# One transformer layer on one core: the normalised rows of the mixing step in one tile per token half, and the operands of the branch products in those same places

## The chip, the cores and the metric

The kernel runs on one core of a Trainium2 chip. What counts is the device time of one execution in microseconds (us), and the time of the kernel before is the median of three runs. In the profile PE is TensorE (PEld its weight loads), DVE is VectorE, ACT is ScalarE, and SP is the queue that issues all DMAs here.

## The reference, cut to what matters

One layer with 1024 tokens and a width of 1024, in float32:

```
h  = x + 1/2 * SwiGLU_1(RMSNorm(x))
u  = RMSNorm(h)
[fox q,k,v,f | dsa q,k,v | indexer q,k,w | mem q | gates] = u @ W_in
o_A = forgetting attention (8 heads of 64)      # "fox", branch n = 0
o_B = top-k sparse attention (8 heads of 64)    # "sparse", branch n = 1
o_C = attention to 256 memory tokens (4 heads of 128)   # "mem", branch n = 2
h  = h + W_out( sum_n sigmoid(u W_g_n) * (o_n W_br_n) )
y  = h + 1/2 * SwiGLU_2(RMSNorm(h))
```

The part in question is the third line from the end: the gates (24 column blocks of `u @ W_g`), and the three branch products, in which each o_n has 512 rows and 1024 tokens.

## The kernel before

Each matrix product is made of three: operands are split into a high and a low part in fp32r (`split`, line 230: a copy on ACT writes the high part, a subtraction on DVE the low part), and `mm3` (line 317) adds high x high, high x low and low x high. A weight block comes by `weights` (line 250): a DMA of 512 KB into a staging slot `wS`, of which there are two during the attention and four once `open_more` has opened a second pool, then ACT's cast to `wH` and DVE's subtraction to `wL`. A slot comes free when that subtraction has read it.

The normalised rows u lie turned (features on partitions) in two tiles `uh` and `ul`, each 128 x 8 x 1024, together 64 KB of each partition, in the pool `u`. `norm_rows` (line 301) writes them, `Block.step` (line 336) and the gates read them.

The order of the work is set in the program by `_Flow.run`, which steps generators ("chains") one at a time by an estimated clock, and after that the framework's scheduler places the instructions of each engine. While the attention heads run, at most two at a time, a *filler* chain gives PE work between their steps: first the gates (`Gates.work`, 24 blocks in groups of two, for each group both blocks over the first 512 tokens, then both over the last 512, two steps for each block and half, 96 steps in all), then `fill` (line 1674). When the last gate is done, `fill` releases the pools of the selection, of the gates and of u, opens a pool `o` in their room, and loads the operands of branch 2 with `o_loaded` (line 1332): for k = 0 to 3 the reciprocal sums of the softmax by DMA into `oR`, the unnormalised o by DMA into `wS`, DVE's product of the two, and the split into high and low tiles of the pool `o`. Then `branch` (line 1293) runs the 16 products of branch 2 (tiles `br` in PSUM, four rows of the contraction with three products each, 12 matmuls), each weighted by its gate (`bg`, loaded from `g_s`) on DVE and stored to `mg_s`. Branch 0 follows in the same way once all fox heads are done, and adds what `mg_s` holds (`bm`). Branch 1 needs the last sparse head, so it runs after all heads, in `last_branch` (line 1741), with tiles of a pool `merge`, and writes its sums as split operands (`u2h`, `u2l`) of the product with W_out (`tm`).

How far the filler may run ahead of the heads is set by `pace`:

```
    left = 2 * 24 * 2 - gates_f.n + 40
    def pace():
        return fill_c.n <= min(left * (sum(c.n for c in heads) / total) + PACE, left - RESERVE)
```

with PACE 4 and RESERVE 6. The 40 are the steps of `fill` after the gates: four loads, 16 products, four loads, 16 products. The last six steps are so kept for the time when all heads are done.

Of the kernel before, what the change touches and what calls it, by code (L numbers as in the profile page):

```python
# [19 lines left out]
P = 128  # L20
# [135 lines left out]
def trunk_layer_kernel(  # L156
# [144 lines left out]
    def norm_rows(tp, row, gain, uh, ul, t, free=None, sq=None, **junk):  # L301
# [3 lines left out]
        for c in range(2):  # L305
            pt = free("nT") if free else bank("nT")
            for k in range(4):
                T.transpose(pt[:, k * P:(k + 1) * P], sq[:, (4 * c + k) * P:(4 * c + k + 1) * P], ident)
            keep = fl.t
            hs = uh[:, 4 * c:4 * c + 4, t * P:(t + 1) * P]  # L310
            ls = ul[:, 4 * c:4 * c + 4, t * P:(t + 1) * P]
            split(hs, ls, pt.rearrange("p (k t) -> p k t", k=4))
            if c == 0:
                fl.t = keep
# [7 lines left out]
    class Block:  # L322
# [13 lines left out]
        def step(self, uh, ul, t, consume, after=None):  # L336
# [7 lines left out]
            for k in range(NK):  # L344
                wh, wl = self.ws[k // kper]
                wh, wl = wh[:, k % kper], wl[:, k % kper]
                a, b = [x[:, k, t * P:(t + 1) * P] if not isinstance(x, list) else
                        x[t // 4][:, k, t % 4 * P:(t % 4 + 1) * P] for x in (uh, ul)]
# [12 lines left out]
    def block_chains(blocks, uh, ul, nt, deps=None, after=None):  # L361
        cs = []
        for i, (b, consume) in enumerate(blocks):
            nxt = blocks[i + 1][0] if i + 1 < len(blocks) else after
            order = getattr(consume, "order", range(getattr(consume, "first", 0), nt))
            for t in order:
                cs.append(chain(b.step(uh, ul, t, consume, nxt if t == order[-1] else None),
# [647 lines left out]
    class Gates:  # L1015


        def __init__(self, uh, ul):
            self.u, self.got, self.tp = (uh, ul), {}, None
# [6 lines left out]
        def work(self):  # L1026
            uh, ul = self.u
            self.fetch(0)
            self.fetch(1)
            for d0 in range(0, 24, 2):  # L1030
                for c, d in ((0, d0), (0, d0 + 1), (1, d0), (1, d0 + 1)):
# [5 lines left out]
                    for k in range(NK):  # L1037
                        if k == NK // 2:
                            yield
                        mm3(pt, [(wh[:, k], uh[:, k, sl]), (wh[:, k], ul[:, k, sl]), (wl[:, k], uh[:, k, sl])],  # L1040
                            k == 0, k == NK - 1)
# [251 lines left out]
    def branch(tp, n, os_, first, dst):  # L1293
# [6 lines left out]
        fetch(0)  # L1300
        fetch(1)
        for dp in range(4):
            fetch(dp + 2)
            wh, wl = got.pop(dp)
            for c in range(2):
                for d in (2 * dp, 2 * dp + 1):
# [18 lines left out]
                    else:  # L1325
                        hv, lv = dst[0][c][:, d], dst[1][c][:, d]
# [5 lines left out]
    def o_loaded(op, n, k):  # L1332
# [5 lines left out]
        return weights(o_s[n, k], [P, S], op, "o", 8, f)  # L1338
# [92 lines left out]
    def to_mix(t, free=None):  # L1431
# [3 lines left out]
        return norm_rows(m["np"], ff.h[t], m["gain"], m["uh"], m["ul"], t, free, stage)  # L1435


    def beside(i, y):
        m = mixing
        if i == 5:  # L1440
            m["up"] = pool("u", side="right")
            m["uh"], m["ul"] = [m["up"].tile([P, NK, S], F32R, name=n) for n in ("uh", "ul")]
# [13 lines left out]
        if i == 9:  # L1456
# [3 lines left out]
            m["gates"] = Gates(m["uh"], m["ul"])  # L1460
# [7 lines left out]
    up, uh, ul = mixing["up"], mixing["uh"], mixing["ul"]  # L1468
# [7 lines left out]
    nch = block_chains([(nb, narrow)], uh, ul, NT, [[]] * 4 + [[c] for c in norms])  # L1476
# [178 lines left out]
    chains = block_chains(blocks, uh, ul, NT)  # L1655
# [10 lines left out]
    right = {"up": up}  # L1666
# [7 lines left out]
    def fill():  # L1674
        yield from gates_f.gen
        finish(sel_c)
        sel.release()
        sgp.release()
        up.release()
        op = right["op"] = pool("o", side="right")  # L1680
        os_ = []
        for k in range(4):
            os_.append(o_loaded(op, 2, k))
            yield fl.clk["PE"] + 2.0
        yield from branch(op, 2, os_, True, None)
        os_ = []
        for k in range(4):
            while not foxes[2 * k + 1].done:
                yield fl.clk["PE"] + 1.0
            os_.append(o_loaded(op, 0, k))  # L1690
            yield fl.clk["PE"] + 2.0
        for t in branch(op, 0, os_, False, None):
            if len(b_os) < 4 and sparses[2 * len(b_os) + 1].done:
                b_os.append(o_loaded(op, 1, len(b_os)))
# [41 lines left out]
    up = pool("u2")  # L1736
    uh, ul = zip(*[[up.tile([P, NK, 512], F32R, name=f"u2{w}{c}") for w in "hl"] for c in range(2)])
    uh, ul = list(uh), list(ul)
    tp = pool("merge")

    def last_branch():
        while len(b_os) < 4:
            b_os.append(o_loaded(op, 1, len(b_os)))
# [7 lines left out]
    tp.release()  # L1751
    op.release()
    repartition(8)
# [41 lines left out]
    fl.run(block_chains(blocks, uh, ul, NT, after=Next()), width=4)  # L1795
    up.release()
# [49 lines left out]
```

## Time and profile before

| | |
|---|---|
| median of 3 runs | 2520.55 us (2514.85 to 2521.84) |
| the profiled execution, its own time | 2521.56 us |
| its span, first to last instruction | 2519.5 us |
| PE busy | 2419.0 us (96% of the span) |
| DVE busy | 1619.4 us (64%) |
| ACT busy | 1149.5 us (46%) |
| mean granted TensorE clock | 0.983 |

A row of the timeline gives the start, the length, the engine, the operation with what it writes and reads, and, in brackets, for how long the engine was idle before it and which event ended that. A row of stretches gives the busy time of each engine within a stretch of the span, and the granted TensorE clock there, where 1.00 is 2.4 GHz and 0.50 is 1.2 GHz. The heads and the gates take the span from about 1170 to 1707 us, the last branch lies between 1722 and 1766 us, and the product with W_out follows it.

### The profile page before, as it was taken

To read this page: it belongs to the slowest core of one execution; us is meant where nothing else is said; L and a number is where in the kernel's file an instruction comes from. 1 tells how busy PE (TensorE), PEld (TensorE's weight loads), DVE (VectorE), ACT (ScalarE), POOL (GpSimd) and SP (SyncE) were. 2 spreads that over 40 slices of the span, in tenths; PEclk is the share of its full clock that TensorE was granted. 3 is DMA by queue.
4 is the path that set the end of the run, shared out by engine and by line. 5 is a ranking of instruction groups with operands and counts; after the bars stand their busy time and mean duration, and the time that the engine had idled before them with its cause. 6 is when DMAs were issued, how large, how long until landed. Compare 5 with 4: busy or idle time off the path is not lost.

```text
span 2519.5 us, 31509 instructions
## 1 busy us (share of the span) xinstructions
PE 2419.0 (96%) x11532; PEld 1998.8 (79%) x11532; DVE 1619.4 (64%) x3162; ACT 1149.5 (46%) x1918; POOL 2.2 (0%) x40
## 2 busy tenths in 40 slices
PE   6999999999999999989999997999999999999998
PEld 5888888888788777777787886888777888888887
DVE  7665555488776788675565456787368555554885
ACT  6433333333443476768854554543144333333332
POOL 0000000000000000000000000000000000000000
PEclk9999999999999999999999998999999999999999
DMA  4323222484345434444554525757413222225743
GB/s 135 122 96 117 93 91 76 159 309 141 131 137 161 153 106 137 137 155 148 149 158 131 142 89 168 236 186 249 160 67 92 84 92 76 84 86 191 266 150 130
DMA packets 300922, 352.15 MB, mean 140 GB/s; under 512 B 19896, under 2 KB 202840, under 8 KB 300768
## 3 DMA queue, kind: packets, MB, share of 16 engines
q1 hardware_dynamic: 300768, 350.15, 43.5%
q8 instruction: 90, 1.47, 0.2%
q14 instruction: 64, 0.52, 0.1%
HBM read 255.51 MB, written 93.54 MB: 139 GB/s over the span
## 4 chain that ended last, share of the span: by engine, by line
PE 74%; DVE 11%; ACT 6%; DMA 6%; issue 3%; SPq 0%; ACTq 0%; DVEq 0%
PE gx L51 18%; PE gy L51 14%; PE tm L51 8%; PE dx L51 7%; PE gate L51 7%; PE dy L51 7%; PE br L51 3%; PE po L51 3%; ACT junk L51 2%; PE sp L51 2%; DVE wL L51 2%; PE pT L51 2%; DMA wS<-in_ffn_w_down 1%; PE nar L51 1%; PE kv L51 1%
## 5 line engine op out<-in xcount | busy, mean ns | idle before, releaser
L51 ACT CAST wH<-wS 128x1024 fp32r<-128x1024 f32 (+1 forms) x230 | 217.0, 949 | 300.3 <-PE gy L51 76.4
L51 DVE TENSOR_TENSOR wL<-wS,wH 128x1024 fp32r<-128x1024 f32 (+1 forms) x230 | 250.6, 1095 | 108.7 <-ACT wH L51 105.2
L51 PE MATMUL gx<-th,wH 128*128 128x512 f32 x704 | 222.7, 398 | 10.3 <-ACT wH L51 6.2
L51 PE MATMUL gy<-th,wH 128*128 128x512 f32 x704 | 221.1, 395 | 5.3 <-DVE th L51 3.5
L51 PE MATMUL gx<-raw,wH 128*128 128x512 f32 x704 | 217.0, 389 | 0.6 <-DVE gu L51 0.6
L51 ACT ACTIVATE junk<-wk,sn 128x384 bf16<-128x384 f32 (+5 forms) x186 | 164.3, 883 | 67.2 <-DVE sn L51 58.3
L51 PEld LDWEIGHTS gx<-th,wH 128*128 128x128 f32 x704 | 134.7, 192 | 40.5 <-ACT wH L51 7.4
L51 DVE TENSOR_TENSOR pl<-pT,ph 128x512 fp32r<-128x512 f32 (+1 forms) x176 | 109.8, 638 | 86.8 <-ACT ph L51 85.3
L51 ACT CAST wH<-S 128x1024 fp32r<-128x1024 f32 x88 | 92.2, 1052 | 158.5 <-PE gy L51 150.5
L51 PEld LDWEIGHTS gy<-th,wH 128*128 128x128 f32 x704 | 133.7, 191 | 34.8 <-DVE th L51 4.4
L51 PE MATMUL gate<-uh,wH 128*128 128x512 f32 x384 | 156.6, 408 | 0.0
L51 DVE TENSOR_TENSOR gu<-gu,gy 128x512 f32<-128x512 f32 x88 | 60.3, 686 | 148.1 <-PE gy L51 105.2
L51 DVE TENSOR_TENSOR wL<-S,wH 128x1024 fp32r<-128x1024 f32 x88 | 107.4, 1223 | 73.9 <-ACT wH L51 73.9
L51 PEld LDWEIGHTS gx<-raw,wH 128*128 128x128 f32 x704 | 132.0, 188 | 28.6 <-DVE gu L51 1.1
L51 PE MATMUL gate<-ul,wH 128*128 128x512 f32 x384 | 153.1, 399 | 0.0
L51 PE MATMUL gate<-uh,wL 128*128 128x512 f32 x384 | 152.3, 397 | 0.0
L51 PE MATMUL tm<-wH,uh 128*128 128x512 f32 x368 | 148.5, 405 | 3.3 <-ACT wH L51 3.3
L51 PE MATMUL tm<-wL,uh 128*128 128x512 f32 x368 | 146.1, 397 | 1.0 <-DVE wL L51 0.5
L51 PE MATMUL tm<-wH,ul 128*128 128x512 f32 x368 | 145.7, 396 | 0.0
L51 PE MATMUL dx<-wH 128*128 128x512 f32 x352 | 138.1, 392 | 2.7 <-DVE rows L51 2.6
L51 PE MATMUL gx<-th,wL 128*128 128x512 f32 x352 | 138.9, 395 | 0.6 <-DVE wL L51 0.5
L51 PE MATMUL gy<-th,wL 128*128 128x512 f32 x352 | 138.7, 394 | 0.0
(282 smaller groups left out, 5528.3 us busy)
## 6 DMA issues: line engine op xcount, KB each, us to landing
wS<-in_ffn_w_down SPq DMA_DIRECT2D x70, 512.0 KB
wS<-in_w_in SPq DMA_DIRECT2D x48, 512.0 KB
wS<-in_ffn_w_gate SPq DMA_DIRECT2D x46, 512.0 KB
wS<-in_ffn_w_up SPq DMA_DIRECT2D x44, 512.0 KB
hid_s<-gu SPq DMA_DIRECT2D x44, 512.0 KB
a<-hid_s SPq DMA_DIRECT2D x30, 512.0 KB
g_s<-sg SPq DMA_DIRECT2D x48, 256.0 KB
bg<-g_s SPq DMA_DIRECT2D x48, 256.0 KB
```

The source lines that it names most:

```text
L51: return fn(*a, **k)
```

## The change

- u lies in two tiles, `u0` for tokens 0 to 511 and `u1` for tokens 512 to 1023, each with both parts (128 x 2 x 8 x 512). A class `Rows` hands out the pieces that readers and writers took before.
- `Rows.again(c)` takes the place of half c a second time, as a tile 128 x 4 x 2 x 1024 for the four high and four low operands of a branch.
- `fill` counts the steps of the gates. After step 92 (the last two blocks over tokens 0 to 511 are done, and four steps over `u1` are left) it finishes the selection, releases its pool, opens the pool `o` and takes the place of `u0`. From there on each of the last four gate steps is followed by one `o_loaded` of branch 2, and the last of these by the first weight block of the branch. Branch 0's operands go to the place of `u1`, branch 1's to that of `u0` again. The loads of branch 2 are no steps of their own any more, and `pace` is as before.
- `branch` yields between its first and second weight block.
- The last branch uses the pool `o` for `bg` and `bm` instead of a pool `merge`; its result goes to a `Rows` pair, and the pools `o`, `sgp` and `u` are released after it.

```diff
+    class Rows:
+        def __init__(self, rp):
+            self.rp = rp
+            self.t = [rp.tile([P, 2, NK, 512], F32R, tag=f"u{c}", name=f"u{c}", bufs=1) for c in range(2)]
...
+        def again(self, c):
+            t = self.rp.tile([P, 4, 2, S], F32R, tag=f"u{c}", name="o", bufs=1)
+            return iter([(t[:, k, 0], t[:, k, 1]) for k in range(4)])
...
         fetch(0)
+        yield
         fetch(1)
...
-    def o_loaded(op, n, k):
+    def o_loaded(op, n, k, place):
+        keep = fl.t, fl.last
         f = op.tile([P, S], F32, tag="oR", name="oR", bufs=2)
...
-        return weights(o_s[n, k], [P, S], op, "o", 8, f)
+        hi, lo = next(place)
+        v = slot([P, S], F32, "wS")
+        load(v, o_s[n, k])
+        V.tensor_mul(v, v, f)
+        split(hi, lo, v)
+        fl.t, fl.last = keep
+        return hi, lo
...
     def fill():
-        yield from gates_f.gen
-        finish(sel_c)
-        sel.release()
-        sgp.release()
-        up.release()
-        op = right["op"] = pool("o", side="right")
-        os_ = []
-        for k in range(4):
-            os_.append(o_loaded(op, 2, k))
-            yield fl.clk["PE"] + 2.0
-        yield from branch(op, 2, os_, True, None)
+        n, os_ = gates_f.n, []
+        for t in gates_f.gen:
+            n += 1
+            if n == 2 * 24 * 2 - 4:
+                finish(sel_c)
+                sel.release()
+                op = right["op"] = pool("o", side="right")
+                first, places = branch(op, 2, os_, True, None), u.again(0)
+            if n >= 2 * 24 * 2 - 4 and len(os_) < 4:
+                os_.append(o_loaded(op, 2, len(os_), places))
+                if len(os_) == 4:
+                    next(first)
+            yield t
+        yield from first
...
-        yield from branch(tp, 1, b_os, False, (uh, ul))
+        yield from branch(op, 1, b_os, False, u2)
...
-    tp.release()
     op.release()
+    sgp.release()
+    up.release()
```

The instructions of each engine are the same in number and kind; their order is the same up to the last gates, and differs from there to the product with W_out.

The first place is DVE's order where the operands of branch 2 are made. Here `wS<-wS,oR` is the product with the reciprocal sums, `pl` the low part of a head's probabilities, `wL` the low part of a weight block or operand, `o` the operand's low part in its new place, `bg<-bg,br` the first use of a branch product. Before, from the last `pl` ahead of the first branch product:

```order
L51 TENSOR_TENSOR pl<-pT,ph 128x512
L51 RECIPROCAL sums<-sums 128x8
L51 TENSOR_TENSOR wS<-wS,oR 128x1024 x2
L51 TENSOR_TENSOR wL<-wS,wH 128x1024 x4
L51 SCALAR_TENSOR_TENSOR bg<-bg,br 128x512
L51 TENSOR_TENSOR wL<-wS,wH 128x1024
L51 SCALAR_TENSOR_TENSOR bg<-bg,br 128x512 x2
```

Changed, from the first operand on (the first two products with the sums lie 17 and 7 `pl` ahead of it):

```order
L51 TENSOR_TENSOR o<-wS,o 128x1024
L51 TENSOR_TENSOR pl<-pT,ph 128x512
L51 TENSOR_TENSOR pl<-pT,ph 128x384
L51 TENSOR_TENSOR o<-wS,o 128x1024
L51 TENSOR_TENSOR wS<-wS,oR 128x1024 x2
L51 TENSOR_TENSOR o<-wS,o 128x1024
L51 TENSOR_TENSOR pl<-pT,ph 128x384
L51 TENSOR_TENSOR pl<-pT,ph 128x512
L51 TENSOR_TENSOR o<-wS,o 128x1024
L51 TENSOR_TENSOR os<-po,lo 64x512
L51 TENSOR_TENSOR pl<-pT,ph 128x512
L51 TENSOR_TENSOR wL<-wS,wH 128x1024
```

The same operations stood together between the last gate and the first branch product; now they stand between the heads' own operations while the last four gate steps run on PE.

The second place is PE's order where the heads end. `po` are the last products of the last head, `rT` its sums, `br` a branch product. Before:

```order
L51 MATMUL rT<-ident,sums 8x128
L51 MATMUL br<-wH 128x512
L51 MATMUL br<-wL,wH 128x512
L51 MATMUL po<-pl,vs 128x256 x2
L51 MATMUL po<-ph,vs 128x256
L51 MATMUL po<-ph,vs 128x128
L51 MATMUL po<-pl,vs 128x256
L51 MATMUL po<-pl,vs 128x128
L51 MATMUL br<-wH,wL 128x512
```

Changed:

```order
L51 MATMUL rT<-ident,sums 8x128
L51 MATMUL br<-o,wH 128x512
L51 MATMUL po<-pl,vs 128x256 x2
L51 MATMUL po<-ph,vs 128x256
L51 MATMUL po<-ph,vs 128x128
L51 MATMUL po<-pl,vs 128x256
L51 MATMUL po<-pl,vs 128x128
L51 MATMUL br<-o,wH 128x512
```

From `rT` to the first `tm` there were 252 `br` matmuls, which is 21 tiles of 12; now there are 216, which is 18. Sixteen of them are branch 1, so five tiles of branch 0 were left behind the heads, and now two are.

The third place is SP's order at the same point, where the last operand of branch 1 (`wS<-o_s`) and the weights of branch 1 (`wS<-in_w_branch`) are loaded. Before:

```order
L176 DMA o_s<-os 64x512
L173 DMA oR<-r_s 64x1024
L176 DMA mg_s<-bg 128x512
L173 DMA wS<-o_s 128x1024
L173 DMA bm<-mg_s 128x512
L176 DMA mg_s<-bg 128x512
L173 DMA bg<-g_s 128x512
L173 DMA bm<-mg_s 128x512
L173 DMA wS<-in_w_branch 128x4x256
```

Changed:

```order
L176 DMA o_s<-os 64x512
L173 DMA oR<-r_s 64x1024
L173 DMA wS<-o_s 128x1024
L176 DMA mg_s<-bg 128x512
L173 DMA wS<-in_w_branch 128x4x256
L176 DMA mg_s<-bg 128x512
L173 DMA wS<-in_w_branch 128x4x256 x2
```

The first weight block stands behind one store of a branch product instead of two, and three blocks stand before any further `bg`.

## Rows read from the trace of the kernel before

**Rows 1.** Stretches from the last gates to the first branch products: the stretch and its length, busy time (and instructions) of PE, PEld, DVE, ACT and POOL, then the granted clock, the share of the DMA engines and GB/s.

```profile
1500.00:1525.00 25.00, 25.00 (x153) 21.84 (x152) 9.24 (x23) 10.64 (x25) 0.00 (x0) 1.00 0.14 48
1525.00:1545.00 20.00, 13.59 (x84) 11.41 (x82) 17.58 (x45) 13.37 (x28) 0.00 (x0) 0.92 0.53 151
1545.00:1557.00 12.00, 1.36 (x3) 1.00 (x4) 5.67 (x7) 4.18 (x7) 0.00 (x0) 0.50 0.81 262
1557.00:1600.00 43.00, 41.63 (x212) 34.74 (x211) 27.61 (x41) 15.56 (x23) 0.00 (x0) 0.94 0.78 242
```

**Rows 2.** PE's timeline: the end of the 92nd gate step, the end of the last gate, the three waits behind it, and the first head operation after the first 36 branch matmuls.

```profile
1507.91 0.39 PE L51 MATMUL gate<-uh,wL 128*128 128x512 f32 x1
...
1529.90 0.39 PE L51 MATMUL gate<-uh,wL 128*128 128x512 f32 x1
...
1541.59 0.63 PE L51 MATMUL po<-ph,vs 128*128 128x256 f32 x2 [3.53 <-ACT ph L51]
1545.24 0.79 PE L51 MATMUL po<-pl,vs 128*128 128x256 f32 x2 [3.03 <-DVE pl L51]
1556.43 0.79 PE L51 MATMUL br<-wH 128*128 128x512 f32 x1 [10.40 <-ACT wH L51]
...
1567.70 0.60 PE L51 MATMUL pT<-ident,ns 128*128 128x128 f32 x4
```

**Rows 3.** SP's queue in the same stretch: start, time to issue, what is loaded.

```profile
1531.82 0.92 SPq L173 DMA_DIRECT2D oR<-r_s  x2
...
1541.58 1.46 SPq L173 DMA_DIRECT2D wS<-o_s  x2
...
1551.58 1.59 SPq L173 DMA_DIRECT2D wS<-in_w_branch  x2
```

**Rows 4.** DVE's and, last, ACT's timeline in the same stretch.

```profile
1537.47 2.34 DVE L51 TENSOR_TENSOR wS<-wS,oR 128x1024 f32<-128x1024 f32 x2
1540.34 2.34 DVE L51 TENSOR_TENSOR wL<-wS,wH 128x1024 fp32r<-128x1024 f32 x2
...
1547.87 2.55 DVE L51 TENSOR_TENSOR wS<-wS,oR 128x1024 f32<-128x1024 f32 x2 [2.57 <-DMA wS<-o_s]
...
1555.34 1.04 ACT L51 CAST wH<-wS 128x1024 fp32r<-128x1024 f32 x1 [3.84 <-DMA wS<-in_w_branch]
```

**Rows 5.** Pieces of the chain of waits, start and length, that give the time of PE's work in steps: a gate step, transposes, products with the values, scores.

```profile
1508.30 0.44 PE pT L51 x4
1508.74 0.48 PE po L51 x4
...
1518.69 1.27 PE sp L51 x8
...
1521.28 2.76 PE gate L51 x12
```

**Rows 6.** ACT's timeline at the 92nd gate step: the gate's tanh.

```profile
1508.34 0.60 ACT L51 ACTIVATE sg<-gate 128x512 f32<-128x512 f32 x1 [2.64 <-PE gate L51]
```

**Rows 7.** PE's timeline where the heads end: the last product of the last head, and the first matmul of branch 1.

```profile
1708.02 0.39 PE L51 MATMUL po<-pl,vs 128*128 128x256 f32 x2
...
1722.60 0.50 PE L51 MATMUL br<-wH 128*128 128x512 f32 x1 [0.96 <-ACT wH L51]
```

**Rows 8.** SP's queue behind it: the last head's output stored and loaded again, and the first weights of branch 1.

```profile
1709.78 0.45 SPq L176 DMA_DIRECT2D o_s<-os  x1
...
1712.76 0.65 SPq L173 DMA_DIRECT2D wS<-o_s  x1
...
1716.28 0.46 SPq L173 DMA_DIRECT2D wS<-in_w_branch  x1
```

**Rows 9.** DVE's timeline there: the product with the sums, and the first use of a product of branch 1.

```profile
1717.30 1.23 DVE L51 TENSOR_TENSOR wS<-wS,oR 128x1024 f32<-128x1024 f32 x1 [0.38 <-DMA wS<-o_s]
...
1730.33 0.68 DVE L51 SCALAR_TENSOR_TENSOR bg<-bg,br 128x512 f32<-128x512 f32 x1
```

**Rows 10.** ACT's timeline there: the high part of the last operand, and of the first weight block.

```profile
1718.56 1.05 ACT L51 CAST wH<-wS 128x1024 fp32r<-128x1024 f32 x1 [9.53 <-DVE wS L51]
1721.50 1.04 ACT L51 CAST wH<-wS 128x1024 fp32r<-128x1024 f32 x1 [1.88 <-DMA wS<-in_w_branch]
```

**Rows 11.** PE's timeline at the end of branch 1: its last matmul, the two waits in the product with W_out, and the first matmul that takes 0.39 us again.

```profile
1766.06 0.39 PE L51 MATMUL br<-wH,wL 128*128 128x512 f32 x1
...
1773.21 0.49 PE L51 MATMUL tm<-wH,u2h 128*128 128x512 f32 x1 [2.68 <-ACT wH L51]
1774.73 0.80 PE L51 MATMUL tm<-wL,u2h 128*128 128x512 f32 x1 [1.03 <-DVE wL L51]
...
1780.82 0.39 PE L51 MATMUL tm<-wH,u2h 128*128 128x512 f32 x1
```

**Rows 12.** DVE's timeline at the same place: the last product of branch 1, and behind it the low part of W_out's fourth block.

```profile
1772.87 0.68 DVE L51 SCALAR_TENSOR_TENSOR bg<-bg,br 128x512 f32<-128x512 f32 x1
1773.46 1.22 DVE L51 TENSOR_TENSOR wL<-wS,wH 128x1024 fp32r<-128x1024 f32 x1
```

**Rows 13.** Stretches with the granted clock (columns as in the first group): two around the clock's return after the wait at the gates, and the one at and after the wait at W_out.

```profile
1560.00:1562.00 2.00, 2.00 (x6) 1.61 (x5) 1.16 (x1) 0.00 (x0) 0.00 (x0) 0.50 0.39 121
1562.00:1564.00 2.00, 2.00 (x9) 1.60 (x9) 1.41 (x2) 1.05 (x1) 0.00 (x0) 0.93 0.87 248
...
1774.00:1780.00 6.00, 5.26 (x12) 4.18 (x13) 1.97 (x3) 0.63 (x1) 0.00 (x0) 0.50 0.65 222
```

More of the change, by code (lines that the diff above doesn't have):

```diff
@@ L334, in fetch, with step @@
                     self.ready[j] = fl.arrival()
-        def step(self, uh, ul, t, consume, after=None):
+        def step(self, u, t, consume, after=None):
             self.fetch()
@@ L359, in col_srcs, with block_chains @@
         ]
-    def block_chains(blocks, uh, ul, nt, deps=None, after=None):
+    def block_chains(blocks, u, nt, deps=None, after=None):
         cs = []
@@ L366, in block_chains @@
             for t in order:
-                cs.append(chain(b.step(uh, ul, t, consume, nxt if t == order[-1] else None),
+                cs.append(chain(b.step(u, t, consume, nxt if t == order[-1] else None),
                                 deps[t] if deps and i == 0 else getattr(consume, "deps", ())))
@@ L1441, in beside @@
             m["up"] = pool("u", side="right")
-            m["uh"], m["ul"] = [m["up"].tile([P, NK, S], F32R, name=n) for n in ("uh", "ul")]
+            m["u"] = Rows(m["up"])
             m["np"] = pool("norm2")
@@ L1665, in trunk_layer_kernel @@
     masks = []
-    right = {"up": up}
+    right = {}
     def finish(c):
@@ L1689, in fill @@
                 yield fl.clk["PE"] + 1.0
-            os_.append(o_loaded(op, 0, k))
+            os_.append(o_loaded(op, 0, k, places))
             yield fl.clk["PE"] + 2.0
+        right["places"] = u.again(0)
         for t in branch(op, 0, os_, False, None):
             if len(b_os) < 4 and sparses[2 * len(b_os) + 1].done:
-                b_os.append(o_loaded(op, 1, len(b_os)))
+                b_os.append(o_loaded(op, 1, len(b_os), right["places"]))
             yield t
@@ L1735, in trunk_layer_kernel @@
     wx = more["pool"]
[L1736 to L1739, printed above, removed]
+    up2 = pool("u2")
+    u2 = Rows(up2)
     def last_branch():
         while len(b_os) < 4:
-            b_os.append(o_loaded(op, 1, len(b_os)))
+            b_os.append(o_loaded(op, 1, len(b_os), right["places"]))
         yield fl.clk["PE"] + 8.0
         yield lambda: fill_c.done
-        yield from branch(tp, 1, b_os, False, (uh, ul))
+        yield from branch(op, 1, b_os, False, u2)
     fl.run([chain(last_branch())], filler=fill_c)
@@ L1794, in trunk_layer_kernel @@
     blocks = [(Block(None, col_srcs(w_out, i * 512, 512), 512, 4), f) for i, f in enumerate((residual, normed_rows))]
-    fl.run(block_chains(blocks, uh, ul, NT, after=Next()), width=4)
-    up.release()
+    fl.run(block_chains(blocks, u2, NT, after=Next()), width=4)
+    up2.release()
     combos.open_high()
```

35 lines of the change are left out of this document (18 added, 17 removed).

## The prediction

> **What bounds the kernel now.** I read the stretches first. PE is busy 25.00 of 25 us while the last gates run, then only 13.59 of 20 and 1.36 of 12, and then nearly full again [rows 1]. So the place to look at is the 32 us between the last gates and the first branch products. PE's timeline shows three waits there, 3.53, 3.03 and 10.40 us long, 16.96 us together [rows 2]. The reader is to see what each waits for: a high part from ACT, a low part from DVE, and then the first weights of branch 2.
>
> SP's and DVE's timelines show why. The last gate ends at 1530.1 [rows 2], and only then may the pool of the operands open: the sums are issued at 1531.82 [rows 3], DVE's products with them run from 1537.47, 5.65 us later, and their casts and subtractions follow. Only the subtractions free the two staging slots, so the next two operands are issued at 1541.58 [rows 3] and multiplied from 1547.87, 6.29 us later [rows 4], and the weights, again in the same slots, come at 1551.58 and are cast at 1555.34, 3.76 us later [rows 3, 4]. That is three loads, one behind the other, 26 us from the last gate to the first branch matmul at 1556.43. The heads cover about 9 us of it. They can't cover more: PE takes its instructions in order, and DVE's low parts for the heads stand between the operands' products.
>
> The waits cost the clock as well. In 1545 to 1557 the granted clock is 0.50, the level of 1.2 GHz, and it is back only after 1562 [rows 1, 13]. The 36 branch matmuls from 1556.43 take until 1567.70 [rows 2], 11.3 us, where 12 take 2.76 us at the full clock [rows 5] and 36 would take 8.3. So another 3.0 us go there. The loss at the gates is 16.96 + 3.0 = **20.0 us**.
>
> The second place is the end of the heads. The last head's last product ends at 1708.4. Its output goes out to DRAM (issued 1709.78), comes back (issued 1712.76), is multiplied at 1717.30 and cast at 1718.56. The first weights of branch 1 are issued at 1716.28 and cast at 1721.50 [rows 7 to 10]. All that takes 14 us, and five tiles of branch 0, 5 x 2.76 = 13.8 us less the two matmuls already done, lie under it, so that PE waits 0.96 us alone [rows 7].
>
> The third place is the product with W_out: branch 1 ends at 1766.3, PE does 18 matmuls, then waits 2.68 and 1.03 us [rows 11], and runs at clock 0.50 until 1780.8 [rows 11, 13]. Fourteen matmuls in 6.1 us instead of 3.2 are 2.9 us. That loss is 3.71 + 2.9 = 6.6 us. It comes from DVE, which first uses a product of branch 1 at 1730.33 [rows 9], 7.7 us after PE began it, where a tile takes 2.76. DVE is thus 5 us late, and ends its last one at 1773.5 [rows 12], with the low part of W_out's fourth block behind it in order.
>
> **The change, part by part.** *u in two tiles.* The same instructions on the same sizes, in the same order up to the last gates. I cost it at nothing. It needs no cover.
>
> *The operands of branch 2 from gate step 92 on.* The sums and the first two operands are loaded well before, as the order of DVE shows. What remains starts when `u0` is dead, at 1508.1 [rows 2]. Then follow the step's tanh on ACT (0.60) [rows 6], the cast (1.05) [rows 10] and the subtraction (1.17, half of 2.34) [rows 4], which frees a slot at 1511.0. The third operand's load takes between 4.54 us (1712.76 to 1717.30) [rows 8, 9] and 6.29 us. The DMA engines are at a share of 0.14 there [rows 1], against 0.53 to 0.81 where the 6.29 was seen, so I take the lower: 1515.5. The fourth comes one subtraction later, 1516.7; product 1517.9; subtraction of the third 1519.0; weights 3.76 us later, 1522.8; cast 1523.9; low part 1525.1. With 6.29 for each of these loads it is 1529.4.
>
> PE's cover: between step 92 and the first branch matmul the new order has four gate steps, 25 transposes, 28 products with values and 8 scores: 4 x 2.76 + 25 x 0.11 + 28 x 0.12 + 8 x 0.16 = 18.4 us [rows 5], so it gets there at 1526.5. That is 1.4 us behind the low part, or 2.9 us ahead of it at the other end. DVE's products now stand between the heads' low parts, but each of these is used a gate step later, 2.76 us, about what one late load costs. I put **1.5 us** of new waits here, half of the worse end. Removed: 20.0. Balance 18.5.
>
> *The four steps fewer.* `pace` still leaves the last six steps for after the heads, but `fill` has four steps fewer, so two tiles of branch 0 are left there, not five. The three tiles have not gone; they run between the heads, and PE's total is the same. But they no longer cover the chain at the end of the heads. Call the end of the last head T. The operand is loaded at T + 4.4, multiplied at T + 8.9, cast from T + 10.2 to T + 11.2 [rows 7 to 10]. The weights stand behind one store instead of two: the first tile ends at T + 2.5, two DVE operations of 0.7 us make T + 4.0 [rows 9], the store goes behind the operand's load, the weights at T + 5.4. They come 5.2 us later, as before (1716.28 to 1721.50), at T + 10.6, and ACT casts them behind the operand, until T + 12.2. PE's 23 matmuls end at T + 5.2. So it waits 7.0 us where it waited 0.96: **+6.0 us**. Without the queue in front of them the weights could come 1 us sooner; with DMA as loaded as at the gates, 2 us later.
>
> Such a wait takes the clock with it: behind the 3.71 us at W_out it was 0.50 until 1780.8 and cost 2.9 us [rows 11, 13]; I add **+2.9 us**. The Trainium skill speaks against this part of the change too: "TensorE: Matmul & The Clock Gate", section "Why this matters for your kernels", tells to leave no idle gaps between bursts of matmuls, since a gap sends the array back to half its clock. The trace agrees at both places. Without that rule and that row the sum would be 2.9 us lower.
>
> The same skill prices a load otherwise than these rows: by "DMA: Bandwidth & Descriptors", section "Anatomy of one DMA", 2.0 us and the bytes at 436 GB/s, fitted on another issuing engine, 512 KB would be an estimated 3.2 us, and the wait behind the heads about 5.7 us. The rows say 4.5 to 6.3, and I stay with them.
>
> *The exit.* DVE's first use of branch 1 has the low parts of three weight blocks ahead of it in both orders. In the new one SP issues blocks two and three right behind the second store, at T + 7.1 and T + 7.6; with some 6 us for a load among others and its casts, the third low part is done at T + 16.5. PE's first tile, at half clock (12 x 0.43), ends at T + 17.3. DVE is then 0.7 us late instead of 5. Its tempo is (1772.87 - 1730.33) / 15 = 2.84 us a tile [rows 9, 12] against PE's 2.76, so it ends some 2 us behind PE instead of 6.6, and W_out's fourth low part, 0.6 + 1.2 us later, comes about when PE has done its 18 matmuls (4.1 us). The 6.6 us go almost wholly: **-6.0 us**. The other end is that they stay.
>
> *Pools released later, `bg` and `bm` from the pool `o`.* Three buffers each, as before. Nothing waits for the pools but the loads of h, behind which PE has eight banks of room.
>
> **Sum.** -20.0 + 1.5 + 6.0 + 2.9 - 6.0 = -15.6 us against the profiled execution's 2521.56, so **2506.0 us**. That execution lies 1.0 us above the median shown; I don't take that off.
>
> **Rivals.** *The exit keeps its wait* (DVE stays late, since its loads of `bg` bind it): -15.6 + 6.0 = -9.6, 2512.0 us. For it: 2.84 us a tile hardly leaves DVE slack. Against it: it starts 4 us less late.
>
> *Half moves.* One late pair of loads on DVE holds the heads as the first pair did (3.53 + 3.03 = 6.6 us), and the exit keeps its wait: -9.6 + 6.6 = -3.0, 2518.6 us. For it: eight operands of two branches now meet heads that have no spare on DVE.
>
> *Slower: the reload chain is as long as before and its cover at the end is gone.* Place: DVE, in order, from gate step 92 to the first branch product. If loads of 6 us and more come in all three rounds and the heads' low parts stand behind them, the 20.0 us come back as waits between the heads, +8.9 us remain at their end, and the exit keeps its wait: 2521.6 + 8.9 = 2530.5 us. It decides from 11.1 us of new waits on. Against it: at a share of 0.14 the DMA engines are free.
>
> *The change doesn't do what it says*: the place of `u0` comes free only with the last gate. Then only the sums' load is saved, 5.65 us, against 8.9: +3.2, 2524.8 us. Against it: in ACT's order the first cast into the place stands right behind the 92nd step's tanh.
>
> **How the numbers follow.** Forecast 0.50, exit kept 0.22, half moved 0.17, slower 0.07, no early place 0.04. A measurement here tells some 0.3%, 7.6 us, from no change, so the borders are 2513.0 and 2528.1. Faster: 0.49 of the forecast and 0.18 of the exit's case, 0.67. Slower: the slower case and a little of the last, 0.08. Same: 0.25. The low end is the forecast without new waits (1.5), without the fall of the clock (2.9) and with 3 us fewer small waits: 2498. The high end takes in most of the half-moved case: 2519. Left out are the last two cases and the edges, 0.2.
>
> **What would show it.** Right: the first branch matmul at about 1527 instead of 1556, at clock 1.00, no wait over 2 us ahead of it; a PE wait of 5 to 9 us behind the last head with clock 0.50 after it; no wait over 1 us in the product with W_out. Wrong: a `po` or `br` that waits over 6 us for DVE or ACT between the gates and the end of the heads, or a wait at W_out as before.

## The result, and the profile after

The changed kernel takes 2504.07 us (median of 4 runs, 2498.82 to 2505.18) where the kernel before, run beside it, takes 2519.86 us (4 runs, 2514.85 to 2521.84). The ratio is 0.9936, with a 95% interval of 0.9916 to 0.9956: faster, by 16 us, where 2506.0 us was forecast. The profiled execution took 2504.25 us, its span is 2502.2 us, which is 17.3 us less than before.

Three points of the program that both traces have cut the span into four stretches and show where the 17.3 us come from. Before, they are the last product of the last head at 1708.02 us, the last matmul of branch 1 at 1766.06 us [rows 7, 11] and the last matmul of W_out at 1864.7 us; after, 1698.04, 1757.11 and 1848.6 us (rows below). Three tiles of branch 0, of 2.76 us each, now run between the heads and not behind them; the fifth column takes that out.

| stretch | before | after | difference | set right for the three moved tiles | forecast |
|---|---|---|---|---|---|
| start to the last head's end | 1708.0 | 1698.0 | -10.0 | **-18.3** (three tiles more are in it, 3 x 2.76 us) | -18.5 |
| from there to the end of branch 1 | 58.0 | 59.1 | +1.0 | **+9.3** (three tiles fewer) | +8.9 |
| from there to the end of W_out | 98.6 | 91.5 | **-7.1** | | -6.0 |
| the rest | 654.8 | 653.6 | -1.2 | | 0 |

The two rows of matmuls of W_out, before and after; behind the durations stand the first and the last start (the second row counts every product with a tile named u, so its first start lies far ahead):

```profile
L51 PE MATMUL tm<-wH,u2l x128: 388/389/632, 1766.7 to 1864.7; 128*128 128x512 f32 x128
```

```profile
L51 PE MATMUL tm<-wH,u x992: 387/389/775, 740.9 to 1848.6; 128*128 128x512 f32 x199
```

**At the gates.** The stretches of [rows 1] in the trace after, same columns, and behind them three around the clock's return at the end of the heads and one at W_out:

```profile
1500.00:1525.00 25.00, 25.00 (x145) 21.66 (x144) 12.80 (x17) 10.76 (x18) 0.00 (x0) 1.00 0.49 149
1525.00:1545.00 20.00, 17.25 (x90) 14.24 (x89) 14.43 (x30) 11.71 (x23) 0.00 (x0) 0.91 0.56 186
1545.00:1557.00 12.00, 12.00 (x67) 10.12 (x67) 11.74 (x31) 8.60 (x18) 0.00 (x0) 1.00 0.81 257
1557.00:1600.00 43.00, 41.61 (x249) 36.01 (x248) 32.35 (x67) 22.31 (x43) 0.00 (x0) 1.00 0.74 229
...
1714.00:1716.00 2.00, 2.00 (x6) 1.52 (x6) 0.78 (x1) 0.00 (x0) 0.00 (x0) 0.50 1.05 398
1716.00:1718.00 2.00, 2.00 (x9) 1.60 (x8) 1.38 (x2) 0.05 (x1) 0.00 (x0) 0.80 0.12 47
1718.00:1720.00 2.00, 2.00 (x11) 1.65 (x10) 1.24 (x2) 1.53 (x2) 0.00 (x0) 1.00 0.38 129
1757.50:1770.00 12.50, 12.50 (x56) 10.35 (x56) 5.00 (x7) 1.54 (x2) 0.00 (x0) 1.00 0.70 272
```

PE is now busy 17.25 of 20 us and 12.00 of 12 where it was 13.59 and 1.36. Its timeline, where [rows 2] had waits of 3.53, 3.03 and 10.40 us:

```profile
1523.67 0.40 PE L51 MATMUL gate<-u,wL 128*128 128x512 f32 x1
...
1528.31 0.33 PE L51 MATMUL pT<-ident,ns 128*128 128x128 f32 x1 [1.95 <-ACT ns L51]
1529.28 0.69 PE L51 MATMUL pT<-ident,ns 128*128 128x128 f32 x2 [0.64 <-ACT ns L51]
1529.62 1.20 PE L51 MATMUL br<-o,wH 128*128 128x512 f32 x2
```

The first branch product waits for nothing; ahead of it PE waits 1.95 and 0.64 us for a head's exponentials. The chain of the operands, on ACT, SP and DVE (one fence for each engine):

```profile
1508.44 0.60 ACT L51 ACTIVATE sg<-gate 128x512 f32<-128x512 f32 x1 [2.64 <-PE gate L51]
1508.93 1.04 ACT L51 CAST o<-wS 128x1024 fp32r<-128x1024 f32 x1
...
1525.03 1.05 ACT L51 CAST wH<-wS 128x1024 fp32r<-128x1024 f32 x1 [3.39 <-DMA wS<-in_w_branch]
...
1527.76 0.40 ACT L51 ACTIVATE ns<-ns,nmx 128x128 f32<-128x128 f32 x1 [1.19 <-DVE nmx L51]
```

```profile
1511.26 2.52 SPq L173 DMA_DIRECT2D wS<-o_s  x2
...
1519.42 0.39 SPq L173 DMA_DIRECT2D wS<-in_w_branch  x1
```

```profile
1514.53 1.23 DVE L51 TENSOR_TENSOR wS<-wS,oR 128x1024 f32<-128x1024 f32 x1 [1.09 <-DMA wS<-o_s]
1517.03 1.23 DVE L51 TENSOR_TENSOR wS<-wS,oR 128x1024 f32<-128x1024 f32 x1 [1.28 <-DMA wS<-o_s]
...
1526.11 1.22 DVE L51 TENSOR_TENSOR wL<-wS,wH 128x1024 fp32r<-128x1024 f32 x1 [3.33 <-ACT wH L51]
```

The cast into the place of u0 starts right behind the tanh of the 92nd step, and the loads follow as walked through ahead. Only the weights are late: cast 5.6 us after their issue, not 3.76, and the head's maxima `nmx`, for which ACT waits, stand behind their low part on DVE.

**At the heads' end.** PE (answers to [rows 7]), SP [rows 8], ACT [rows 10] and DVE [rows 9]:

```profile
1698.04 0.44 PE L51 MATMUL po<-pl,vs 128*128 128x256 f32 x2
...
1710.38 1.22 PE L51 MATMUL br<-o,wH 128*128 128x512 f32 x2 [6.63 <-ACT wH L51]
1711.83 0.80 PE L51 MATMUL br<-o,wL 128*128 128x512 f32 x1 [0.23 <-DVE wL L51]
```

```profile
1702.21 0.35 SPq L173 DMA_DIRECT2D wS<-o_s  x1
...
1703.08 0.43 SPq L173 DMA_DIRECT2D wS<-in_w_branch  x1
```

```profile
1708.34 1.04 ACT L51 CAST o<-wS 128x1024 fp32r<-128x1024 f32 x1 [9.24 <-DVE wS L51]
1709.29 1.04 ACT L51 CAST wH<-wS 128x1024 fp32r<-128x1024 f32 x1
```

```profile
1713.56 1.23 DVE L51 TENSOR_TENSOR wL<-wS,wH 128x1024 fp32r<-128x1024 f32 x1 [0.23 <-ACT wH L51]
1716.51 0.69 DVE L51 SCALAR_TENSOR_TENSOR bg<-bg,br 128x512 f32<-128x512 f32 x1 [1.72 <-PE br L51]
```

The wait has grown from 0.96 to 6.63 us, and the clock is at 0.50 until some 1716.8 us. But DVE, which was 5 us late at branch 1's start, now waits 1.72 us for PE there.

**At W_out.** PE's first matmul follows the last of branch 1 without a wait, at clock 1.00 (last stretch above), where [rows 11] had 2.68 and 1.03 us:

```profile
1757.11 0.39 PE L51 MATMUL br<-o,wL 128*128 128x512 f32 x1
1757.34 0.39 PE L51 MATMUL tm<-wH,u 128*128 128x512 f32 x1
```

### The profile page after: what moved, and what is told of

Read it like the earlier page. It is cut to its first block, busy times and chain, and to the rows that moved or that the text cites. A ratio compares the mean times of both kernels' runs of the same rounds, so it can differ in the third digit from the quotient of the medians.

```text
span 2502.2 us, 31494 instructions
## 1 busy us (share of the span) xinstructions
PE 2412.6 (96%) x11532; PEld 1995.0 (80%) x11532; DVE 1617.9 (65%) x3162; ACT 1149.1 (46%) x1918; POOL 2.2 (0%) x40
## 4 chain that ended last, share of the span: by engine, by line
PE 74%; DVE 12%; ACT 7%; DMA 4%; issue 3%; SPq 0%; ACTq 0%; DVEq 0%
PE gx L51 19%; PE gy L51 14%; PE dx L51 8%; PE gate L51 7%; PE tm L51 7%; PE dy L51 6%; PE br L51 4%; ACT junk L51 3%; PE po L51 2%; PE sp L51 2%; DVE wL L51 2%; PE pT L51 2%; DMA wS<-in_ffn_w_down 1%; PE nar L51 1%; ACT ns L51 1%
## 5 line engine op out<-in xcount | busy, mean ns | idle before, releaser
L51 ACT CAST wH<-wS 128x1024 fp32r<-128x1024 f32 (+1 forms) x218 | 204.6, 944 | 260.7 <-PE gy L51 78.0
L51 PE MATMUL tm<-wH,u 128*128 128x512 f32 x992 | 319.5, 396 | 3.4 <-ACT wH L51 3.4
L51 DVE TENSOR_TENSOR wL<-wS,wH 128x1024 fp32r<-128x1024 f32 (+1 forms) x218 | 236.2, 1089 | 101.1 <-ACT wH L51 98.8
L51 PE MATMUL gate<-u,wH 128*128 128x512 f32 x768 | 248.9, 401 | 0.0
L51 PEld LDWEIGHTS tm<-wH,u 128*128 128x128 f32 x992 | 187.4, 189 | 42.0 <-ACT wH L51 4.6
L51 PE MATMUL tm<-wL,u 128*128 128x512 f32 x496 | 195.1, 393 | 1.0 <-DVE wL L51 0.8
L51 PEld LDWEIGHTS gate<-u,wH 128*128 128x128 f32 x768 | 140.3, 191 | 24.8 <-DVE u L51 0.2
L51 PE MATMUL gate<-u,wL 128*128 128x512 f32 x384 | 151.7, 395 | 0.0
```

What stands on the lines that cost most here:

```text
L51: return fn(*a, **k)
```

## The experiments

Twelve kernels, each run beside the kernel before. The waits are PE's in the profiled execution: from 1500 us to 15 us behind the first branch matmul, from the last head's end to the end of branch 1, and in W_out. "Tiles left" are those of branch 0 behind the heads. Each kernel has one profiled execution, and it isn't always near the median: e1's and e8's are among their longest (2506.16 and 2506.74 us), e3's and e7's are their shortest (2495.90 and 2493.72), so a difference of a microsecond or two between the waits of two kernels isn't shown by them.

| kernel | median us (range, runs) | ratio to before, 95% | waits: gates / heads' end / W_out |
|---|---|---|---|
| before (5 tiles left) | 2519.86 | 1 | 16.96 / 0.96 / 3.71 |
| the change (2 tiles) | 2504.07 | 0.9936, 0.9916 to 0.9956 | 2.75 / 6.86 / 0 |
| e1, five tiles | 2501.11 (2498.07 to 2506.16, 6) | 0.9933, 0.9919 to 0.9947 | 1.32 / 2.16 / 3.40 |
| e2, before with two tiles | 2518.68 (2513.96 to 2523.11, 12) | 1.0004, 0.9993 to 1.0014 | 17.82 / 7.62 / 0 |
| e3, loads after the last gate (7 tiles) | 2502.01 (2495.90 to 2506.41, 6) | 0.9938, 0.9923 to 0.9953 | 0.52 / 0.52 / 4.26 |
| e4, own pool for the last branch | 2502.01 (2498.49 to 2507.94, 6) | 0.9940, 0.9925 to 0.9954 | 1.25 / 6.60 / 0 |
| e5, place of u1 | 2516.38 (2513.99 to 2518.56, 12) | 0.9991, 0.9981 to 1.0000 | 11.46 / 7.12 / 0 |
| e6, weights first, 2 tiles | 2501.17 (2494.44 to 2504.33, 6) | 0.9927, 0.9911 to 0.9943 | 1.53 / 1.53 / 4.43 |
| e7, weights first, 4 tiles | 2497.63 (2493.72 to 2502.40, 6) | 0.9920, 0.9905 to 0.9934 | 1.77 / 0.16 / 1.77 |
| e8, as e3, weights first, 4 tiles | 2499.27 (2497.11 to 2506.80, 6) | 0.9929, 0.9912 to 0.9946 | 2.42 / 0 / 3.32 |
| e9, 13 unread matmuls | 2502.79 (2499.32 to 2506.10, 5) | 0.9944, 0.9928 to 0.9961 | 1.63 / 3.87 / 0.48 |
| e10, as e7, six buffers | 2497.17 (2494.79 to 2499.77, 5) | 0.9921, 0.9903 to 0.9939 | 1.99 / 0 / 1.02 |
| e11, 26 unread matmuls | 2501.79 (2500.83 to 2503.96, 6) | 0.9932, 0.9919 to 0.9945 | 1.91 / 0.60 / 0 |
| e12, as e8, six buffers | 2501.44 (2498.40 to 2507.56, 6) | 0.9931, 0.9916 to 0.9945 | 1.70 / 0 / 2.14 |

### What the gain at the gates hangs on: e3 and e5

e3 puts the loads back behind the last gate in the program, and keeps the places:

```diff
     def fill():
-        n, os_ = gates_f.n, []
-        for t in gates_f.gen:
...
+        os_ = []
+        yield from gates_f.gen
+        finish(sel_c)
+        sel.release()
+        op = right["op"] = pool("o", side="right")
+        places = u.again(0)
+        for k in range(4):
+            os_.append(o_loaded(op, 2, k, places))
+            yield fl.clk["PE"] + 2.0
+        yield from branch(op, 2, os_, True, None)
```

> The changed kernel, but the operands of branch 2 are loaded after gate step 96 instead of between steps 92 and 96, four steps of their own again; the places and the pool order are those of the change. Theory A (the gain at the gates is the cover of the last four steps): the sums still come early, since the pool o needs no gate's room, but the casts start at the last gate and two rounds of loads follow it, so some 9 to 11 us of the 20 remain as waits of PE between the last gate and the first branch matmul; the end of the heads and W_out are as in the kernel before or better covered: 2508 to 2513 us. Rival D (the early sums are the gain, not the place of u0): below 1 us of difference to the change in that stretch, 2500 to 2505 us. Rival E (neither, the order between heads is): the full loss, about 2520 us.

The waits did not come back; the expectation was wrong. ACT's timeline of e3:

```profile
1506.79 0.60 ACT L51 ACTIVATE sg<-gate 128x512 f32<-128x512 f32 x1 [2.64 <-PE gate L51]
1507.75 1.06 ACT L51 CAST o<-wS 128x1024 fp32r<-128x1024 f32 x1
```

The casts stand behind the 92nd step's tanh although the program emits them four gate steps later: the framework's scheduler, which places the instructions of each engine, takes them forward as far as their place allows. So where the loads are written does not matter here. The time also lies in the range of rival D, which holds that the early sums are the gain and not the place. e5 tests the place itself:

```diff
-                first, places = branch(op, 2, os_, True, None), u.again(0)
+                first, places = branch(op, 2, os_, True, None), u.again(1)
...
-        places = u.again(1)
+        places = u.again(0)
...
-        right["places"] = u.again(0)
+        right["places"] = u.again(1)
```

> The changed kernel with the two places exchanged: branch 2's operands take the place of u1, which the last four gate steps still read, branch 0's that of u0, branch 1's that of u1 again. Everything else, the early pool and the early sums among it, stays. Theory A (the place that is free four gate steps early carries the gain at the gates): the casts can start only behind the last gate, two rounds of loads of 5 to 6 us follow, and PE waits 9 to 13 us between the last gate and the first branch product, part of it at the half clock: 2514 us, 2510 to 2519. Rival B (the gain comes from the early pool and the early sums, not from the place): waits below 4 us there, 2500 to 2506 us, as with the operands' loads behind the last gate.

It took 2516.38 us, as theory A has it (2510 to 2519). ACT, SP and PE of e5:

```profile
1525.92 2.01 ACT L51 CAST o<-wS 128x1024 fp32r<-128x1024 f32 x2 [2.46 <-PE gate L51]
...
1540.34 1.05 ACT L51 CAST wH<-wS 128x1024 fp32r<-128x1024 f32 x1 [3.57 <-DMA wS<-in_w_branch]
```

```profile
1528.26 1.45 SPq L173 DMA_DIRECT2D wS<-o_s  x2
...
1536.86 1.59 SPq L173 DMA_DIRECT2D wS<-in_w_branch  x2
```

```profile
1541.44 1.22 PE L51 MATMUL br<-o,wH 128*128 128x512 f32 x2 [10.40 <-ACT wH L51]
```

With the sums and the pool as early as in the change, but a place that the last four gate steps read, the casts wait for the last gate, two rounds of loads follow, and the wait of 10.40 us is back. Some 13 of the 16 us hang on which half of u the operands take.

### What the cover behind the heads is worth: e1, e2 and e4

```diff
-PACE, RESERVE = 4, 6
+PACE, RESERVE = 4, 9
```

> The changed kernel with RESERVE 9 instead of 6, so that five tiles of branch 0 are left behind the heads, as in the kernel before, instead of two. Theory A (the wait behind the heads is the lost cover, and the wait at W_out went because branch 1 began late and DVE was no longer behind): PE's wait behind the last head falls from 6.6 to about 1 us and the clock stays at 1.00 (-8.6 us), but the weights of branch 1 stand behind more stores again, DVE is late again and the wait at W_out comes back (3.7 us and 2.9 us of clock): about 2502 us. Rival B (the wait at W_out went for another reason than the late start, as the pools or the layout): it stays away, about 2495.5 us. Rival C (the wait behind the heads isn't a matter of cover): no change, 2504 us with the wait in place.

The same line of the kernel before, with 3, leaves two tiles there:

```diff
-PACE, RESERVE = 4, 6
+PACE, RESERVE = 4, 3
```

> The kernel before with RESERVE 3 instead of 6 and nothing else: two tiles of branch 0 are left behind the heads instead of five, and u, its pools and the loads of branch 2 are as they were. Theory A: a wait of 6 to 7 us behind the last head with the clock at 0.50 after it (+8.6 us), no wait at W_out (-6.6 us), the 17 us at the gates unchanged: about 2522 us, 2 us over the kernel before. Rival B: the same wait behind the heads, and the wait at W_out stays, about 2528.5 us. Rival C: no wait behind the heads, about 2520 us.

PE's waits behind the heads and in W_out in e1, then in e2:

```profile
1709.91 1.66 PE L51 MATMUL br<-o,wH 128*128 128x512 f32 x6 [2.16 <-ACT wH L51]
1759.63 0.49 PE L51 MATMUL tm<-wH,u 128*128 128x512 f32 x1 [1.80 <-ACT wH L51]
1761.72 0.50 PE L51 MATMUL tm<-wL,u 128*128 128x512 f32 x1 [1.60 <-DVE wL L51]
```

```profile
1726.69 0.80 PE L51 MATMUL br<-wH 128*128 128x512 f32 x1 [7.39 <-ACT wH L51]
1728.14 0.79 PE L51 MATMUL br<-wH,wL 128*128 128x512 f32 x1 [0.23 <-DVE wL L51]
```

In both programs the cover turns one wait into the other: five tiles give a wait at W_out, two give 7 us behind the heads and none at W_out. e2 has the waits that theory A expects, and costs nothing measurable (ratio 0.9993 to 1.0014); of the times expected for it, those of 2520 and 2522 us are near, 2528.5 is out. e1 is as theory A has it, and its 2501 us can't be told from the change's 2504. So the four steps fewer were no loss, and the change's gain is all at the gates.

```diff
+    mp = pool("merge")
...
-        yield from branch(op, 1, b_os, False, u2)
+        yield from branch(mp, 1, b_os, False, u2)
```

> The changed kernel, with bg and bm of the last branch in a pool of their own again, as before. Theory A: nothing follows from the pool, 2504 us within 2 us, the wait of 6.6 us behind the heads in place and no wait over 1 us at W_out. Rival F (the shared buffers are what keeps the wait at W_out away, as loads of bg start sooner in a pool that is open already): the wait at W_out is back, about 2510 us.

With a pool of its own for `bg` and `bm`, the wait is 6.37 and 0.23 us and the time 2502.01: sharing the pool `o` plays no part.

### What the clock behind the wait costs: e9 and e11

```diff
         yield lambda: fill_c.done
+        pt, (oh, ol) = bank("br"), b_os[2]
+        for i in range(13):
+            T.matmul(pt, oh[:, :P], oh[:, :512], start=i == 0, stop=i == 12)
         yield from branch(op, 1, b_os, False, u2)
```

> The changed kernel with 13 matmuls of 128x512 whose result nobody reads, put between the last product of branch 0 and the first of branch 1: 13 x 0.39 = 5.1 us of work inside PE's wait of 6.63 us behind the heads. Theory A (the half clock behind that wait costs 2.9 us of its own, because PE stood still): the wait that is left is 1.5 to 2.5 us, the granted clock stays at 1.00, branch 1 begins at the same time and ends 2.5 to 3 us sooner, no wait over 1 us at W_out: 2501 us, 2499 to 2503. Rival C (branch 1 is held by DVE or by the loads of bg behind it, so that time won at its start is waited for at W_out): the clock stays at 1.00 and a wait of 2 to 4 us comes back at W_out: 2503 to 2506 us. Rival D (the slow matmuls behind the wait are not the idle time's doing): the clock falls all the same: 2504 us.

Mis-sized: 13 matmuls in a row take 3.11 us, 0.23 us each (0.39 us is the length that the timeline gives for one, which overlaps the next). A wait of 3.87 us was left, and the clock fell all the same; the run decides nothing. e11 has 26 of them.

> As the run with 13 unread matmuls in PE's wait behind the heads, with 26: 13 took 3.11 us there (0.23 us each, the time that a matmul of 128x512 takes in a row of them, not 0.39), left a wait of 3.87 us, and the clock fell to 0.50 again. 26 take 6.1 us and leave less than 1.5 us. Theory A (the idle time brings the half clock, which costs 3.2 us behind the wait of 6.63 us): clock 1.00 from 1700 us on, first 12 matmuls of branch 1 in 2.8 to 3.5 us instead of 6, branch 1 ends 2.5 to 3.2 us sooner after the heads' end than in the changed kernel: 2501 us, 2499 to 2503.5. Rival C (then DVE is late and waits for bg, and a wait of 2 to 4 us comes at W_out): clock 1.00, 2503 to 2506 us. Rival D (the slow matmuls are not the idle time's doing): clock 0.50 there all the same, 2504 us.

PE's timeline and two stretches of e11, then one stretch of e9 for comparison:

```profile
1700.85 0.45 PE L51 MATMUL po<-pl,vs 128*128 128x256 f32 x2
...
1706.44 6.05 PE L51 MATMUL br<-o 128*128 128x512 f32 x26
1712.83 1.19 PE L51 MATMUL br<-o,wH 128*128 128x512 f32 x4 [0.34 <-ACT wH L51]
...
1756.80 0.39 PE L51 MATMUL br<-o,wL 128*128 128x512 f32 x1
```

```profile
1714.00:1716.00 2.00, 1.74 (x8) 1.43 (x8) 1.45 (x2) 1.65 (x2) 0.00 (x0) 1.00 1.06 407
1716.00:1718.00 2.00, 2.00 (x10) 1.68 (x9) 1.12 (x2) 0.00 (x1) 0.00 (x0) 1.00 1.08 394
```

```profile
1716.00:1718.00 2.00, 2.00 (x6) 1.60 (x5) 0.80 (x1) 1.00 (x1) 0.00 (x0) 0.50 1.05 374
```

With PE at work the granted clock stays at 1.00. From the last head's end to the last matmul of branch 1 it is 55.95 us, against 59.07 in the change: 3.1 us less, of which 0.36 because branch 1 begins sooner (11.98 against 12.34 us behind the last head's end). The clock alone is 2.8 us. No wait comes at W_out, so theory A holds; 2501.79 us fits it, but alone it would not be told from 2504.

### Cover and order together: e6, e7, e8, e10 and e12

In e6 branch 1's first weights are loaded ahead of its last operand; e7 has RESERVE 8 besides, e8 is e3's form with RESERVE 3.

```diff
     def last_branch():
+        last = branch(op, 1, b_os, False, u2)
+        next(last)
         while len(b_os) < 4:
...
-        yield from branch(op, 1, b_os, False, u2)
+        yield from last
```

> The changed kernel, with branch 1's first weight block loaded ahead of its last operand instead of behind it; two tiles of branch 0 are still left behind the heads. Theory A (PE's wait of 6.63 us behind the heads is the weights behind the operand in the queue, and DVE's lateness sets the wait at W_out): the chain of the last operand alone is left, cast at 10 to 11 us behind the last head's end, and PE has 5.2 us of branch 0 and 2.1 us of branch 1's first nine matmuls, so it waits 3 to 4 us, no wait at W_out: 2500 us, 2497 to 2504. Rival B (the operand's own way out and back sets the wait, so the weights' place changes nothing): wait of 6 us or more, 2503 to 2506 us.

> As the one before, with RESERVE 8, so that four tiles of branch 0 are left behind the heads. Theory A (cover and chain then meet: 11.0 us of branch 0 and 2.1 us of branch 1's first matmuls against a chain of 11 to 12 us, and DVE is not late at branch 1's start): no wait over 1 us behind the heads, none over 1 us at W_out, clock 1.00 from 1700 us on: 2496 us, 2493 to 2500. Rival C (what is not waited for behind the heads is waited for at W_out, whatever the order of the loads, as with five tiles: 1.80 and 1.60 us): 2500 to 2504 us.

> The loads of branch 2 emitted behind the last gate as steps of their own (this had no wait over 0.4 us at the gates), branch 1's first weights ahead of its last operand, RESERVE 3, so that four tiles are left behind the heads. Theory A (the three places add up: gates without a wait, heads' end covered, no wait at W_out): 2494 us, 2490 to 2498. Rival C (one wait turns into another): 2499 to 2504 us, with a wait over 2 us in one of the three places.

e6 shortens the wait behind the heads to 1.53 us, more than expected, and has 4.43 us at W_out, which neither theory had; its time lies in A's range all the same. e7 lies in A's range; 1.77 us at W_out are left, half of what C expects. e8 misses A's range by 1.3 us, with 2.92 us among the heads and 2.30 and 1.02 at W_out: C's way. What these have in common is seen on DVE in e7:

```profile
1721.18 0.69 DVE L51 SCALAR_TENSOR_TENSOR bg<-bg,br 128x512 f32<-128x512 f32 x1 [0.52 <-DMA bg<-g_s]
1723.70 0.69 DVE L51 SCALAR_TENSOR_TENSOR bg<-bg,br 128x512 f32<-128x512 f32 x1 [0.63 <-DMA bg<-g_s]
...
1744.36 0.69 DVE L51 SCALAR_TENSOR_TENSOR bg<-bg,br 128x512 f32<-128x512 f32 x1 [2.15 <-DMA bg<-g_s]
```

In branch 1 DVE waits for `bg`, whose three buffers come free only behind DVE's own work. The kernel before has four such waits from 1724.5 us on (0.72, 1.06, 1.91 and 2.36 us), the change two of 0.27. Such waits alone don't bring the wait at W_out: e4 has 2.88 us of them (for `bg` and `bm`) and e11 3.13, and neither waits at W_out. e10 and e12 give that branch six buffers, from two pools in turn:

```diff
-    def branch(tp, n, os_, first, dst):
-        got = {}
+    def branch(tp, n, os_, first, dst, more_tp=None):
+        got, more_tp = {}, more_tp or tp
...
+                    tp, more_tp = more_tp, tp
                     g = tp.tile([P, 512], F32, tag="bg", name="bg", bufs=3)
```

> The kernel with branch 1's first weights ahead of its last operand and four tiles left behind the heads, and with six buffers instead of three each for bg and bm in branch 1 (from two pools in turn). Theory A (the waits that DVE still has for bg in branch 1, the longest 2.15 us, come from the three buffers: a load is issued only when DVE has read the buffer's last user): these waits and the 1.77 us at W_out go: 2495.5 us, 2493 to 2498. Rival B (the DMA engines, at a share of 0.88 in that stretch, set the time of the loads): the waits stay, 2497 to 2500 us.

> The loads of branch 2 emitted behind the last gate, branch 1's first weights ahead of its last operand, four tiles left behind the heads, and six buffers for bg and bm in branch 1. With three buffers this kernel took 2499.3 us, with DVE's waits for bg (0.32 to 2.04 us, 5.9 together) and PE's of 2.30 and 1.02 us at W_out. Theory A (the three buffers make both): DVE has no wait over 0.3 us for bg, PE none over 1.1 us at W_out: 2496 us, 2493 to 2498.5. Rival B (something else holds W_out there): 2498.5 to 2502 us with a wait over 2 us at W_out.

In e10 no wait for `bg` is left, at a DMA share of 0.82 (1720 to 1750 us), so the buffers made them; but 2497.17 us is e7's time, and lies in the range of both theories, so that these waits cost time is not shown. Another wait has come, for W_out's first block, whose load is issued at 1734.44 us where e7 issued it at 1721.06 (e10's DVE):

```profile
1741.59 1.22 DVE L51 TENSOR_TENSOR wL<-wS,wH 128x1024 fp32r<-128x1024 f32 x1 [2.41 <-ACT wH L51]
```

e12 took 2501.44 us, as rival B has it, with 2.14 us at W_out; DVE still waits 0.33 and 1.65 us for `bg`. It has also 3.06 us among the heads at 1555.48 us, where a product on DVE waits 4.57 us for an operand of branch 0 and a head's low parts stand behind it:

```profile
1553.13 1.23 DVE L51 TENSOR_TENSOR wS<-wS,oR 128x1024 f32<-128x1024 f32 x1 [4.57 <-DMA wS<-o_s]
```

That is the mechanism of "half moves", at another operand. The order of every engine is the same in e8 up to there, and e8's DVE waits less for the same operand:

```profile
1555.77 1.23 DVE L51 TENSOR_TENSOR wS<-wS,oR 128x1024 f32<-128x1024 f32 x1 [2.02 <-DMA wS<-o_s]
```

From issue to product this load took 7.25 us in e12 (issued 1545.88), 4.69 in e8 and 5.37 in e3, and PE then waited 3.06, 0.55 and 1.18 us. So the size of this wait follows that one load; why it took longer in e12's profiled execution is open. The fastest kernels are e7 and e10; their intervals overlap the change's, so that they are faster than it, by some 4 us by the ratios, is likely and not shown.

## Why the prediction was right

*The gates.* Right in place and cause, and in size by some luck: -18.3 us measured up to the heads' end, -18.5 forecast. The walk held up to the fourth operand (products begin at 1514.53 and 1517.03, forecast 1515.5 and 1516.7), though at the fourth two errors nearly cancel: the loads took 3.27 and 3.57 us from issue to product, where 4.54 was taken, and the fourth was issued at 1513.46, 1.3 us later than the forecast has it, since two low parts of a head stood ahead of the subtraction that frees its slot. The DMA engines were no longer at a share of 0.14 there, but at 0.49 (first stretch above). The weights' load was mis-sized, 5.6 us for 3.76, so that the low part was done at 1527.3, not 1525.1, and the first branch matmul came at 1529.62, not 1526.5. New waits are 2.75 us, not 1.5, and the clock fell once more, to 0.91 over 1525 to 1545. That the total came out alike, with 1.25 us more of new waits, has two reasons, neither of them forecast: the waits among the heads fell from 3.5 to 2.4 us, and the old loss in clock was larger than the 3.0 us taken. By the granted clock it is about 4.3 us (the shortfall times the busy time in the last three stretches of [rows 1]), and 1.6 us now. e5 shows that the place is the cause.

*"u in two tiles" at nothing.* The 92nd step's tanh is at 1508.44 us, 0.1 us from before.

*The wait behind the heads.* 6.63 + 0.23 us, forecast 7.0. The chain held to within a microsecond, counted from the last head's end at 1698.5: operand issued at 3.7 us (forecast 4.4), multiplied at 8.6 (8.9), cast at 9.9 (10.2), weights issued at 4.6 (5.4), cast until 11.9 (12.2). The clock behind it cost 2.8 us by e11, forecast 2.9. The Trainium skill's "TensorE: Matmul & The Clock Gate", section "Why this matters for your kernels", says not to leave gaps between bursts of matmuls; e11, where filling the gap with useless products kept the clock at 1.00, agrees. The Trainium skill's "DMA: Bandwidth & Descriptors", section "Anatomy of one DMA", gave an estimated 3.2 us for such a load. Here the two operands at the gates took 3.27 and 3.57 us from issue to product, near it, at DMA shares of 0.53 and 0.61; the operand behind the heads took 4.9 us at 0.87 and the weights at the gates 5.6 at 0.84. So the measurement bears the estimate out at the lower shares and goes against it at the higher ones, and the 4.5 to 6.3 us that the prediction stayed with were too long for the operands at the gates.

*The exit.* -7.1 us, forecast -6.0, for the reason given: DVE's third low part was done 16.3 us behind the heads' end (forecast 16.5), PE's first tile at 18.0 (17.3), and DVE was not late. What the forecast did not have is that a late DVE frees the three buffers of `bg` late and then waits for the next loads, 6.05 us together behind the heads in the kernel before, 0.54 us after. e10 shows that the three buffers make such waits; how much of the wait at W_out they made before is not shown.

*The rivals.* The exit did not keep its wait, the heads took no wait over 1.95 us at the gates, and the early place is real. The rule that a lost cover costs its length is true only with its counterpart: in e2 the same loss of cover, alone, cost nothing, since W_out's wait went.

*The expectations that failed* are e3's (it took the place in the program for the place in the order), e9's size, W_out in e6 and e7, and e8's and e12's sums of gains.

## What to carry to other kernels

When operands are to be loaded early, ask when the place that they go to is read for the last time: a scheduler that hoists took care of the rest here, and splitting a tile so that a part of it dies earlier can be the whole change. A wait of the bounding engine gives the engine behind it time to catch up, so take a wait away only together with the next one in line (order of loads, cover, buffers), and count both. Check the fall of the clock behind each wait as a cost of its own.

## What the runs showed that was not expected

Kernels with the same order up to about 1575 us have a wait of PE there for a head's output on DVE, of 0.38 us in the change, 0.83 (e6), 1.86 (e9), 2.18 (e11) and 2.35 us (e10) in their profiled executions, and none in e7. A single execution's profile is thus no better than about 2 us at such a place. Behind the wait of 2.16 us in e1 the clock stayed at 1.00; behind 3.87 us in e9 it fell to 0.50, and cost some 1.7 us (13 matmuls in 4.67 us where 13 x 0.23 us is 3.0).
